# A gated linear recurrence: diagonal and five lower levels of the intra-chunk scores as four blocks of 32 keys by 32 queries

## The chip, the cores and the metric

The kernel runs on one core of a Trainium2 chip. The metric is the device time of one execution in microseconds (us). TensorE is written PE here, its weight loads PEld, VectorE DVE, ScalarE ACT, GpSimd POOL and the DMA-issuing engine SP, as the profile writes them.

## What is computed

One decoder layer over 1024 tokens of width 1024: a projection, a gated linear recurrence (HGRN2, 4 heads of 128 by 128) beside sliding-window attention, a gated merge, a layer norm and a mixture of 32 experts. The change lies in the recurrence alone. Per chunk of tokens it needs the scores

```python
def step(state, xs):
    qb, kb, vb, lb_c = xs
    b = jnp.cumsum(lb_c, axis=2)
    o_inter = jnp.einsum('bhtk,bhkv->bhtv', qb * jnp.exp(b), state)
    diff = b[:, :, :, None, :] - b[:, :, None, :, :]
    decay = jnp.exp(jnp.where(tri[:, :, None], diff, -jnp.inf))
    scores = jnp.einsum('bhtk,bhtsk,bhsk->bhts', qb, decay, kb)
    o_intra = jnp.einsum('bhts,bhsv->bhtv', scores, vb)
...
```

Scores exist only for keys that are not later than their query, so the matrix of a chunk (keys by queries) is upper triangular.

## The kernel before

The program has four stages: the attention with its projections (to about 300 us), the recurrence (about 305 to 550 us), the merge with norm and router (to about 800 us), and the experts. Through the attention and the recurrence a second piece of work is woven into PE's order: the stream, which multiplies the remaining columns of the projection as three matmuls of 512 columns each per step (lines 102 to 104). PE's order is written by the program (`pe_order`); the function `weave` puts a piece of the stream ahead of each group of the recurrence, by a fixed share of the stream and not by any clock. DVE, ACT, POOL and SP are ordered by a scheduler in these two stages.

The recurrence (`hgrn`) works on chunks of 128 tokens, eight of them. The triangle of a chunk is built by levels h = 64, 32, ..., 1 and a diagonal. At level h the chunk is cut into pairs of h tokens; the scores of the later half's queries against the earlier half's keys are one product of two decayed operands, which stand side by side in one tile e of 128 (channels) by 4 heads by 128 (tokens). `prep_level` makes e: on ACT two exponentials (lines 562 and 565), on DVE a subtraction, two multiplications and an addition (lines 564, 566, 569, 570); the addition turns the tile of sums `hl` into that of the next level, so that the levels of a chunk are made one after the other, h = 1 first. `level` multiplies: for each head e by itself on PE into a PSUM tile `pb` (keys on partitions, 4 heads by 128 queries), and then copies what belongs to the level into the scores `st` (tile `hst`, set to zero by POOL). Level 64 multiplies one block of 64 by 64 per head, level 32 two blocks of 32 by 32 per head (lines 580, 581), whose results lie in partitions 0 to 31 and 64 to 95, and ACT copies them. The levels 16, 8, 4, 2, 1 multiply 128 by 128 per head (line 583), and one DVE copy under a mask takes what counts (line 590). The diagonal does the same with keys and queries as they are (lines 549, 550).

Operands are in full 32-bit floating point, for which one matmul of the program stands as two MATMUL rows in the trace.

A group is prepared two groups before it is multiplied (`ahead = 2`). There are five `pb` buffers in PSUM, so a copy that is late holds one of five. After the levels come the decayed keys, the output and the state of the chunk (`decay`, `output`, `state`), which read the finished scores.

Of the kernel before, what the change touches and what calls it, by code (L numbers as in the profile page):

```python
# [7 lines left out]
I32 = mybir.dt.int32  # L8
# [14 lines left out]

LAST = (15, 23, 31)
ORDER = tuple(e for e in range(NE) if e not in LAST) + LAST
LEVELS = (64, 32, 16, 8, 4, 2, 1)


def constants():
# [12 lines left out]
    parts["tok"] = np.arange(8)[None, :] * 128 + r - FAR  # L42
    for h in LEVELS[2:]:
        parts[f"lev{h}"] = (r // (2 * h) == c // (2 * h)) & (r % (2 * h) < h) & (c % (2 * h) >= h)
# [16 lines left out]
class Builder:  # L61
# [457 lines left out]
    def hgrn(self):  # L519
# [3 lines left out]
        nc = self.nc  # L523
        mm = nc.tensor.matmul
        V = {}
        lo, hi = WHERE[f"lev{LEVELS[2]}"][0], WHERE["lev1"][1]
        lev = self.tile([128, hi - lo], F32, "lev", 1)
        nc.sync.dma_start(lev, self.a["const"][:, lo:hi])

        def mask(name):  # L530
            m = self.c("ident") if name == 0 else lev[:, WHERE[f"lev{name}"][0] - lo:WHERE[f"lev{name}"][1] - lo]
            return m.bitcast(I32)[:, None, :].to_broadcast([128, 4, 128])

        def load(n):
            t0 = slice(n * 128, n * 128 + 128)
            for nm, src in (("hl", self.hl[:, :, t0]), ("hk", self.hk[:, :, t0]), ("hq", self.hq[:, :, t0]),
# [2 lines left out]
                V[nm, n] = self.tile([128, 4, 128], F32, nm, 2)  # L539
                nc.sync.dma_start(V[nm, n], src)  # L540

        def prep_diag(n):
            V["st", n] = self.tile([128, 4, 128], F32, "hst", 1)
            nc.gpsimd.memset(V["st", n], 0.0)

        def diag(n):
            pp = self.bank("pb", (128, 4, 128))
            for hd in range(4):
                mm(pp[:, hd], V["hk", n][:, hd], V["hq", n][:, hd], start=True, stop=True)
            nc.vector.copy_predicated(V["st", n], mask(0), pp)  # L550

        def prep_level(n, h):
            q, kT, b = V["hq", n], V["hk", n], V["hl", n]
            ns = 4 * (64 // h)

            def view(t):
                return t.rearrange("p h (s two x) -> p (h s) two x", two=2, x=h)

            e = self.tile([128, 4, 128], F32, "hE", 2)
            ev, bv, qv, kv = view(e), view(b), view(q), view(kT)  # L560
            ref = bv[:, :, 0, h - 1:h].to_broadcast([128, ns, h])
            nc.scalar.activation(ev[:, :, 1], bv[:, :, 1], AF.Exp)
            if h > 1:
                nc.vector.tensor_sub(ev[:, :, 0], ref, bv[:, :, 0])
                nc.scalar.activation(ev[:, :, 0], ev[:, :, 0], AF.Exp)
                nc.vector.tensor_mul(ev[:, :, 0], ev[:, :, 0], kv[:, :, 0])
            else:
                nc.gpsimd.tensor_copy(ev[:, :, 0], kv[:, :, 0])
            nc.vector.tensor_mul(ev[:, :, 1], ev[:, :, 1], qv[:, :, 1])
            nc.vector.tensor_add(bv[:, :, 1], bv[:, :, 1], ref)  # L570
            V["e", n, h] = e

        def level(n, h):
            e, st = V.pop(("e", n, h)), V["st", n]
            pp = self.bank("pb", (128, 4, 128))
            for hd in range(4):
                if h == 64:
                    mm(pp[0:64, hd, 64:128], e[:, hd, 0:64], e[:, hd, 64:128], start=True, stop=True)
                elif h == 32:
                    mm(pp[0:32, hd, 32:64], e[:, hd, 0:32], e[:, hd, 32:64], start=True, stop=True)  # L580
                    mm(pp[64:96, hd, 96:128], e[:, hd, 64:96], e[:, hd, 96:128], start=True, stop=True)
                else:
                    mm(pp[:, hd], e[:, hd], e[:, hd], start=True, stop=True)
            if h == 64:
                nc.scalar.copy(st[0:64, :, 64:128], pp[0:64, :, 64:128])
            elif h == 32:
                nc.scalar.copy(st[0:32, :, 32:64], pp[0:32, :, 32:64])
                nc.scalar.copy(st[64:96, :, 96:128], pp[64:96, :, 96:128])
            else:
                nc.vector.copy_predicated(st, mask(h), pp)  # L590

        def prep_decay(n):
            b = V["hl", n]
# [56 lines left out]
        for n in range(8):  # L650
            at = 11 * n
            groups.append((at, lambda n=n: prep_diag(n), lambda n=n: diag(n)))
            for i, h in enumerate(reversed(LEVELS)):
                pre = lambda n=n, h=h: prep_level(n, h)
                if i == 3 and n < 7:
                    pre = lambda n=n, h=h: (load(n + 1), prep_level(n, h))
                groups.append((at + 1 + i, pre, lambda n=n, h=h: level(n, h)))
            groups.append((at + 8, lambda n=n: prep_decay(n), lambda n=n: decay(n)))
            groups.append((at + 10.5, none, lambda n=n: state(n)))
            groups.append((at + 9.6, none, lambda n=n: output(n)))  # L660
            groups.append((at + 13.5, none, lambda n=n: out(n)))
# [392 lines left out]
    def column(self, t, e):  # L1054

        x = ORDER[e]
        return t[:, x:x + 1]
# [35 lines left out]
    def fetch(self, first=False):  # L1093
# [4 lines left out]
        e, m, k = self.pieces[n]  # L1098
        x = ORDER[e]
        if m == "w_d":  # L1100
# [397 lines left out]
```

## Time and profile before

| | us |
|---|---|
| median of 3 runs | 1424.0 (1423.0 to 1429.07) |
| the profiled execution's own time | 1423.78 |
| its span, first to last instruction | 1421.9 |
| PE busy | 1359.1 (96%) |
| DVE busy | 1058.2 (74%) |
| ACT busy | 792.3 (56%) |

The span is 1.9 us shorter than the time of the same execution. Busy time counts an instruction from start to end; on PE and DVE the next one starts before the last has ended, so two starts stand closer than one duration, and what an instruction costs its engine is read from starts.

### The profile page before, as it was taken

What the parts mean: (1) busy time and instruction counts of PE and PEld (TensorE: products, weight loads), DVE (VectorE), ACT (ScalarE), POOL (GpSimd) and SP (SyncE); (2) the same over time, 40 slices, a digit from 0 to 9 for tenths busy, and PEclk for the clock granted to TensorE, in tenths of its full rate; (3) what the DMA queues carried; (4) which work ended last, traced back from release to release, by engine and by line L of the source; (5) the groups of instructions that cost most, each with busy time, mean ns of one, the idle gap of its engine ahead of it and who ended that gap; (6) DMA issues with size and microseconds to landing.
All of it is one profiled execution on the core that took longest, in us unless ns stands there. A gap on an engine that the chain in (4) does not pass through costs nothing. (4 is left out here: it accounts for less than half of the span.)

```text
span 1421.9 us, 20450 instructions
## 1 busy us (share of the span) xinstructions
PE 1359.1 (96%) x7162; PEld 1128.3 (79%) x7162; DVE 1058.2 (74%) x1654; ACT 792.3 (56%) x1282; POOL 239.6 (17%) x160
## 2 busy tenths in 40 slices
PE   7999999999999999999998999999999999999844
PEld 5888899988888888788787888888888888888721
DVE  4268977876666764857747889999999999999635
ACT  4367555434444442412201778888888888888533
POOL 0001221210010000410001112222222222222123
PEclk9999999999999999999999999999999999999967
DMA  6124223253334323774557899999999999999972
GB/s 254 56 89 156 88 92 105 67 173 116 126 108 136 111 88 103 240 252 137 174 195 277 314 361 369 370 359 349 360 349 359 357 359 360 360 359 361 370 264 95
DMA packets 142554, 327.68 MB, mean 230 GB/s; under 512 B 18614, under 2 KB 59702, under 8 KB 142448
## 3 DMA queue, kind: packets, MB, share of 16 engines
q1 hardware_dynamic: 132800, 308.78, 60.4%
q0 software_dynamic: 9648, 17.57, 4.8%
q8 instruction: 57, 0.93, 0.3%
q14 instruction: 49, 0.40, 0.1%
HBM read 291.43 MB, written 52.43 MB: 242 GB/s over the span
## 5 line engine op out<-in xcount | busy, mean ns | idle before, releaser
L98 DVE TENSOR_TENSOR el<-er,eh 128x1024 fp32r<-128x1024 f32 x368 | 436.5, 1221 | 53.7 <-ACT eh L97 38.1
L97 ACT CAST eh<-er 128x1024 fp32r<-128x1024 f32 x368 | 368.9, 1053 | 100.6 <-PE mm L103 83.5
L102 PE MATMUL mm<-xh,wh 128*128 128x512 f32 x480 | 198.3, 413 | 8.3 <-ACT wh L97 7.3
L102 PE MATMUL mm<-eh,xh 128*128 128x512 f32 x496 | 196.4, 396 | 0.0
L103 PE MATMUL mm<-el,xh 128*128 128x512 f32 x496 | 196.2, 395 | 0.0
L104 PE MATMUL mm<-eh,xl 128*128 128x512 f32 x496 | 196.1, 395 | 0.0
L103 PE MATMUL mm<-xl,wh 128*128 128x512 f32 x480 | 188.4, 393 | 0.8 <-DVE xl L98 0.8
L104 PE MATMUL mm<-xh,wl 128*128 128x512 f32 x480 | 189.0, 394 | 0.0
L104 PEld LDWEIGHTS mm<-eh,xl 128*128 128x128 f32 x496 | 93.2, 188 | 22.6
L103 PEld LDWEIGHTS mm<-el,xh 128*128 128x128 f32 x496 | 93.2, 188 | 22.3
L102 PEld LDWEIGHTS mm<-eh,xh 128*128 128x128 f32 x496 | 93.2, 188 | 22.3
L102 PEld LDWEIGHTS mm<-xh,wh 128*128 128x128 f32 x480 | 91.1, 190 | 24.2 <-ACT wh L97 7.3
L104 PEld LDWEIGHTS mm<-xh,wl 128*128 128x128 f32 x480 | 90.6, 189 | 20.6 <-DVE wl L98 0.8
L1064 POOL DMA_INDIRECT xg<-x1d,gi x32 | 58.1, 1814 | 279.3 <-PE pb L1127 236.3
L103 PEld LDWEIGHTS mm<-xl,wh 128*128 128x128 f32 x480 | 91.1, 190 | 16.0 <-DVE xl L98 1.4
L102 PE MATMUL mm<-eh,hth 128*128 128x512 f32 x240 | 100.2, 418 | 0.0
L1068 POOL DMA_INDIRECT zd<-y,gi x29 | 69.9, 2411 | 156.5 <-ACT y L1218 156.5
L104 PE MATMUL mm<-eh,htl 128*128 128x512 f32 x240 | 94.8, 395 | 0.0
L103 PE MATMUL mm<-el,hth 128*128 128x512 f32 x240 | 94.8, 395 | 0.0
L102 PE MATMUL mm<-wh,xh 128*128 128x256 f32 x256 | 73.1, 285 | 0.0
L104 PE MATMUL mm<-wh,xl 128*128 128x256 f32 x256 | 72.4, 283 | 0.0
L103 PE MATMUL mm<-wl,xh 128*128 128x256 f32 x256 | 72.4, 283 | 0.0
(257 smaller groups left out, 2566.6 us busy)
## 6 DMA issues: line engine op xcount, KB each, us to landing
er<-w_g SPq DMA_DIRECT2D x128, 512.0 KB, 12.5
er<-w_u SPq DMA_DIRECT2D x128, 512.0 KB, 12.5
er<-w_d SPq DMA_DIRECT2D x128, 512.0 KB, 12.0
wr<-w_in SPq DMA_DIRECT2D x38, 512.0 KB, 4.4
gated<-st SPq DMA_DIRECT2D x32, 256.0 KB, 2.1
st<-gated SPq DMA_DIRECT2D x32, 256.0 KB, 2.7
xr<-xt SPq DMA_DIRECT2D x8, 512.0 KB, 7.6
wab<-w_a SPq DMA_DIRECT2D x16, 256.0 KB, 3.7
```

Of the source, the lines that this page charges most:

```text
L97: self.nc.scalar.copy(hi, src)
L98: (eng or self.nc.vector).tensor_sub(lo, src, hi.bitcast(F32))
L102: mm(out, lh, rh, start=start, stop=False)
L103: mm(out, lh, rl, start=False, stop=False)
L104: mm(out, ll, rh, start=False, stop=stop)
L1064: self.nc.gpsimd.indirect_dma_start(to, None, rows, bass.IndirectOffsetOnAxis(ap=self.column(self.gi, e), axis=0), bounds_check=T - 1, oob ...
L1068: self.nc.gpsimd.indirect_dma_start(self.zd, bass.IndirectOffsetOnAxis(ap=idx, axis=0), y, None, bounds_check=T - 1, oob_is_err=False, com ...
```

## The change

The diagonal and the levels 16 to 1 no longer multiply 128 by 128 per head, but four blocks of 32 keys by 32 queries on the matrix's diagonal; no score of these levels lies outside those blocks. Each block writes its own 32 partitions of `pb`. The copy under the mask is cut the same way: four copies of 32 partitions by 4 heads by 32 queries.

```diff
+RUNS = [slice(b, b + 32) for b in range(0, 128, 32)]
...
-            return m.bitcast(I32)[:, None, :].to_broadcast([128, 4, 128])
+            return m.bitcast(I32)
+
+        def keep(st, name, pp):
+            for b in RUNS:
+                m = mask(name)[b, b][:, None, :].to_broadcast([32, 4, 32])
+                nc.vector.copy_predicated(st[b, :, b], m, pp[b, :, b])
...
+        def blocks(out, l, r):
+
+            for b in RUNS:
+                mm(out[b, b], l[:, b], r[:, b], start=True, stop=True)
...
-                mm(pp[:, hd], V["hk", n][:, hd], V["hq", n][:, hd], start=True, stop=True)
-            nc.vector.copy_predicated(V["st", n], mask(0), pp)
+                blocks(pp[:, hd], V["hk", n][:, hd], V["hq", n][:, hd])
+            keep(V["st", n], 0, pp)
...
-                    mm(pp[:, hd], e[:, hd], e[:, hd], start=True, stop=True)
+                    blocks(pp[:, hd], e[:, hd], e[:, hd])
...
-                nc.vector.copy_predicated(st, mask(h), pp)
+                keep(st, h, pp)
```

On PE the order of the groups is the same; a group of four matmuls has become one of sixteen. The first rows are PE's before, around a level of the first chunk, the second those of the change (line numbers have moved).

```order
L102 MATMUL mm<-xh,wh 128x512
L103 MATMUL mm<-xl,wh 128x512
L104 MATMUL mm<-xh,wl 128x512
L583 MATMUL pb<-hE 128x128 x4
L102 MATMUL mm<-xh,wh 128x512
```

```order
L103 MATMUL mm<-xh,wh 128x512
L104 MATMUL mm<-xl,wh 128x512
L105 MATMUL mm<-xh,wl 128x512
L551 MATMUL pb<-hE 32x32 x16
L103 MATMUL mm<-xh,wh 128x512
```

This is so at all 48 places; nothing of the stream has moved past a group.

On DVE the scheduler also shifts copies against the work for later levels. These are DVE's rows in the third chunk before, from the end of the preparation of level 2 on, and then those of the change at the same place (`hst` is written by the copies, `hE` is e, `st` is the stream's).

```order
L566 TENSOR_TENSOR hE<-hE,hk 128x128x2
L550 COPY_PREDICATED hst<-const,pb 128x512
L564 TENSOR_TENSOR hE<-hl 128x64x4
L590 COPY_PREDICATED hst<-lev,pb 128x512
L508 TENSOR_SCALAR st<-st 128x512
L566 TENSOR_TENSOR hE<-hE,hk 128x64x4
L569 TENSOR_TENSOR hE<-hE,hq 128x64x4
L570 TENSOR_TENSOR hl<-hl 128x64x4
L564 TENSOR_TENSOR hE<-hl 128x32x8
L590 COPY_PREDICATED hst<-lev,pb 128x512
```

```order
L577 TENSOR_TENSOR hE<-hE,hk 128x128x2
L538 COPY_PREDICATED hst<-const,pb 32x4x32 x4
L538 COPY_PREDICATED hst<-lev,pb 32x4x32 x4
L509 TENSOR_SCALAR st<-st 128x512
L575 TENSOR_TENSOR hE<-hl 128x64x4
L580 TENSOR_TENSOR hE<-hE,hq 128x64x4
L581 TENSOR_TENSOR hl<-hl 128x64x4
L577 TENSOR_TENSOR hE<-hE,hk 128x64x4
L538 COPY_PREDICATED hst<-lev,pb 32x4x32 x4
L575 TENSOR_TENSOR hE<-hl 128x32x8
```

The copies of level 1 now stand ahead of the first DVE step for level 4 (the tile of 64 pieces of 4), where one copy stood behind it.

## Rows read from the trace of the kernel before

**Rows 1.** The page: span, busy time by engine, granted clock in 40 slices.

```profile
span 1421.9 us, 20450 instructions
...
PE 1359.1 (96%) x7162; PEld 1128.3 (79%) x7162; DVE 1058.2 (74%) x1654; ACT 792.3 (56%) x1282; POOL 239.6 (17%) x160
...
PEclk9999999999999999999999999999999999999967
```

**Rows 2.** Stretches: length, busy PE, PEld, DVE, ACT, POOL (counts), clock, DMA share, GB/s.

```profile
350.00:380.00 30.00, 30.00 (x192) 25.67 (x191) 19.75 (x49) 13.47 (x30) 1.38 (x2) 1.00 0.40 124
...
550.00:600.00 50.00, 47.06 (x205) 36.71 (x205) 35.49 (x44) 16.70 (x20) 15.21 (x7) 1.00 0.66 208
800.00:1300.00 500.00, 500.00 (x2319) 407.35 (x2318) 452.55 (x442) 409.53 (x499) 116.06 (x54) 1.00 0.99 360
```

**Rows 3.** PE's waits from 290 to 560 us: in total, times, longest.

```profile
PE mm L102 <- ACT st L507: 0.7, 1, 0.7
```

**Rows 4.** Groups by line: count, then busy us, mean ns, and idle before.

```profile
L583 PE MATMUL pb<-hE 128*128 128x128 f32 x320 | 42.3, 275 | 0.0
...
L590 DVE COPY_PREDICATED hst<-lev,pb 128x512 f32<-128x512 int32 x40 | 29.6, 741 | 1.0 <-PE pb L583 0.8
...
L344 DVE COPY_PREDICATED as<-const,sc 128x256 f32<-128x256 int32 x28 | 10.9, 442 | 3.2 <-ACT as L340 3.1
```

**Rows 5.** Timeline of PE around a level of 128 by 128: start, length, instruction.

```profile
307.74 0.40 PE L104 MATMUL mm<-xh,wl 128*128 128x512 f32 x1
307.98 1.06 PE L583 MATMUL pb<-hE 128*128 128x128 f32 x8
...
309.11 0.39 PE L103 MATMUL mm<-xl,wh 128*128 128x512 f32 x1
309.34 0.39 PE L104 MATMUL mm<-xh,wl 128*128 128x512 f32 x1
```

**Rows 6.** Timeline of PE around a level 32.

```profile
321.15 0.39 PE L104 MATMUL mm<-xh,wl 128*128 128x512 f32 x1
...
321.52 0.20 PE L580 MATMUL pb<-hE 128*32 128x32 f32 x1
...
321.71 0.20 PE L580 MATMUL pb<-hE 128*32 128x32 f32 x1
321.72 0.20 PE L581 MATMUL pb<-hE 128*32 128x32 f32 x1
321.84 0.50 PE L102 MATMUL mm<-xh,wh 128*128 128x512 f32 x1
322.18 0.39 PE L103 MATMUL mm<-xl,wh 128*128 128x512 f32 x1
```

**Rows 7.** Timeline of DVE: copies under a mask, and 128-element operations on PSUM.

```profile
191.98 0.77 DVE L344 COPY_PREDICATED as<-const,sc 128x256 f32<-128x256 int32 x2
...
308.83 0.73 DVE L550 COPY_PREDICATED hst<-const,pb 128x512 f32<-128x512 int32 x1
309.45 0.41 DVE L564 TENSOR_TENSOR hE<-hl 128x256 f32<-128x256 f32 x1
...
364.04 1.13 DVE L642 SCALAR_TENSOR_TENSOR ho<-pb,hss,hg 128x128 f32<-128x128 f32 x4 [1.13 <-POOL hss L679]
```

**Rows 8.** Timeline of DVE and PE where the third chunk's levels begin.

```profile
365.08 0.41 DVE L569 TENSOR_TENSOR hE<-hE,hq 128x256 f32<-128x256 f32 x1
...
367.45 0.42 DVE L570 TENSOR_TENSOR hl<-hl 128x256 f32<-128x256 f32 x1
367.79 0.42 DVE L566 TENSOR_TENSOR hE<-hE,hk 128x256 f32<-128x256 f32 x1
...
366.52 1.06 PE L583 MATMUL pb<-hE 128*128 128x128 f32 x8
...
369.48 0.72 PE L583 MATMUL pb<-hE 128*128 128x128 f32 x5
```

**Rows 9.** PE's waits from 550 to 610 us, where the merge begins.

```profile
PE mm L104 <- DVE l L98: 2.2, 5, 0.5
```

## The prediction, made before the changed kernel ran

> **What bounds the kernel now.** I read the page first: PE is busy for 96% of a span of 1421.9 us, at a granted clock of nine tenths or more in all but the last two slices [rows 1]. An average says nothing of the recurrence, so the stretches come next. In 30 us inside it PE is busy for all 30.00, DVE for 19.75, ACT for 13.47, and the DMA engines for 0.40 of the time [rows 2]. Of that 30 us a chunk takes nearly the whole (eight chunks in some 245 us). Then PE's waits: between 290 and 560 us it waits once for another engine, for 0.7 us [rows 3]. The stage is bound by PE alone, and what its blocks cost is what the stage is worth. The reader should look at starts, not at durations: a MATMUL row of the levels is 275 ns long on average [rows 4], but eight of them take 1.06 us together [rows 5].
>
> What comes behind the recurrence is read from two stretches. From 800 to 1300 us PE is busy without a gap and the DMA engines to 0.99 [rows 2]. The experts' weights are fetched by steps of the merge, not at a time of their own, so a recurrence that ends earlier moves all of this earlier by as much.
>
> **PE: what a block costs now.** The last plain matmul before a level starts at 307.74, the second one behind it at 309.11 [rows 5]: 1.37 us. Two plain matmuls of the stream start 0.23 us apart (309.11 and 309.34 [rows 5]); two such steps belong to the stream, so the block costs 1.37 - 0.46 = 0.91 us. Line 583 has 320 rows [rows 4], eight to a block: 40 blocks, and the eight diagonals have the same shape. 48 blocks x 0.91 = 43.7 us of the stage.
>
> **PE: what a block will cost.** The trace of before has a near relative: level 32, which already multiplies 32 by 32 with 128 channels. Its two blocks per head write different partitions, so they use different 32 columns of the array. Measured the same way, from 321.15 to 322.18 [rows 6], it is 1.03 - 0.46 = 0.57 us for sixteen rows. How these sixteen run decides the case. Rows of line 580 alone go from 321.52 (its second) to 321.71 (its eighth): 0.19 / 6 = 0.032 us from one to the next in the same columns. The last of line 581 starts 0.01 us behind that of line 580 [rows 6]. So two column groups run side by side, each at 0.032 us a row. The eight rows of one column group thus take 8 x 0.032 = 0.26 us, and the remaining 0.31 us of the 0.57 are paid once, for entering and leaving the narrow shape.
>
> The changed block has 32 rows in four column groups: again eight rows in each. If four run side by side as two do, the block takes the 0.57 us of level 32 and two more offsets of 0.01: 0.59 us. It saves 0.91 - 0.59 = 0.32 us, and 48 x 0.32 = **15.4 us** on PE.
>
> What no row of before shows is three or four column groups at once. The bounds: if the offsets between groups cost nothing, 0.57, a saving of 16.3 us; if only two run at a time, eight more steps of 0.032, 0.83 us, a saving of 0.08 x 48 = 3.8 us. I take the first end, since the offset of 0.01 us leaves room for four within 0.032.
>
> The Trainium skill speaks against the change at this place: TensorEngine Tiling, Instruction Overhead, says that each matmul carries about 60 cycles, so that a free dimension of 1 costs as much as one of 60, and warns against taking a tiling factor from a dimension that is already small. As an estimate from that page, 60 cycles at 2.4 GHz are 25 ns, and 32 rows at 25 ns with the 0.31 us would be 1.11 us, 0.20 more than now. The rows of level 32 disagree in part: sixteen starts in 0.25 us are 16 ns each, less than the page's floor, though 32 ns within one column group.
>
> **DVE: what is added.** One copy of 512 elements a partition keeps DVE for 309.45 - 308.83 = 0.62 us [rows 7]; it becomes four of 128. Two copies of 256 take 0.77 us together [rows 7], one of them 0.44 by itself [rows 4], so the second starts 0.33 behind the first. From 256 to 512 it is 0.29 us, 1.13 ns an element; 128 elements would then take 0.33 - 0.145 = 0.19. From above, four operations of 128 elements from PSUM take 1.13 us at line 642 [rows 7], 0.26 from start to start. So four copies take 0.76 to 1.04 us, 0.14 to 0.42 more than now, or 48 times that, 7 to 20 us of DVE work. I take 0.8. The cover is DVE's idle third: about 10 us of each 30 [rows 2]; per chunk 6 x 0.14 to 0.42 = 0.8 to 2.5 us are added, and the chunk becomes 1.9 us shorter.
>
> An average cover can still fail where the levels follow each other closely. There DVE has per level four steps of 0.34 us (367.45 to 367.79 [rows 8]) and the copy: 1.36 + 0.8 = 2.16 us, 2.4 at the upper bound. Between two levels PE has six or nine plain matmuls: 6 x 0.23 + 0.59 = 1.97 or 9 x 0.23 + 0.59 = 2.66, on average 2.3. The two keep step; what guards PE is the lead with which e is ready. It is shortest in the third chunk: level 1 is ready at 365.49 and used at 366.52, level 2 at 368.21 and 369.48 [rows 8], leads of 1.0 and 1.3 us. Level 1 has one block and one copy between it and the output of the chunk before, which DVE waits for: its lead shrinks by 0.32 + 0.18 = 0.5 us; that of level 2 by twice as much, to 0.3. At the later levels of that chunk and in the other chunks the leads are longer. So DVE should not stop PE, or by a few tenths here and there; I charge **0.5 us** in all. A stall would first show at level 2 of a chunk.
>
> The scheduler's shifts on DVE cost nothing of their own: where copies now stand ahead of work for level 4, PE still has a whole level before it needs that. ACT, POOL and the bytes moved are unchanged; SP issues the same DMAs. The five PSUM buffers are held 0.2 us longer in turns of over 2 us. The semaphore at a block's end is still one.
>
> **The sum.** -15.4 + 0.5 = -14.9 us. The profiled execution took 1423.78 us (its span is 1421.9), 0.2 less than the median of 1424.0; 1424.0 - 14.9 = 1409.1, and I say **1409.0**. With the bounds of the block and of the small stalls (0 to 3) this case spans 1406 to 1413.
>
> **The rivals.** *Two column groups at a time.* The pattern of level 32 would be all the array does: 0.83 us a block, 1424.0 - 3.8 = 1420, within what can be measured. For it: no row shows more than two. Against it: nothing in the offset of 0.01 us says that two is an end.
>
> *One after another.* If the rows overlap in level 32 only because its two blocks lie 64 partitions apart, and neighbours do not, the 32 rows take 32 x 0.032 = 1.02 us and the block 1.33, 0.42 more than now: 48 x 0.42 = 20 us, **1444**. It decides from the point where a block costs more than 0.91, that is, above 19 ns a row. The rule of TensorEngine Tiling in the Trainium skill would end on this side too, by its estimate at 0.20 x 48 = 9.6 us slower. Against both: 16 ns a row in level 32 [rows 6].
>
> *DVE becomes the bound.* If copies of 32 partitions do not follow each other closely but each runs its full length of 0.44 us (the length of a 256-element copy [rows 4]), four take 1.77, a level 3.1 us against PE's 2.3. Over six such groups that is 4.8 us a chunk less a lead of about 2: some 2.8 x 8 = 22 us against 15.4 won, 1431. From about 1.3 us for four copies on the gain begins to shrink. Against it: two copies of 256 overlap [rows 7].
>
> *The gain stops at the merge.* From 550 to 600 us DMA is at 0.66 and PE waits 2.2 us for halves of weights [rows 2, 9]. Should those loads not start earlier with the recurrence's end, some of the 15 us turns into waits there; all of it would give 1424, a third 1414. Against it: the waits are at most 0.5 us each, and the loads are issued by groups of the recurrence.
>
> That the change does not do what it says can be left out: the order shows sixteen 32 by 32 matmuls at all 48 places.
>
> **The chances.** About 0.5%, 7 us, can be told from no change. Forecast 0.68; part of it lost to DVE or at the merge (1413 to 1418) 0.09; two at a time 0.11; all lost at the merge 0.04; one after another 0.05; DVE as the bound 0.03. Faster by over 0.5% (below 1417) is the forecast and most of the second: 0.76. Slower is the last two: 0.08. The rest, 0.16, is no change. For 8 in 10 the range must take in the forecast, the partial losses and half of the two-at-a-time case: 1405 to 1420; the forecast's own is 1406 to 1413.
>
> **What would show it.** In the changed profile the 128x32 rows of a block should start in four staggered lines, 8 ns or so apart, with 0.03 us within one line; the plain matmuls before and behind a block should stand 1.05 us apart by the measure above (0.59 + 0.46). The recurrence's PE should still be full, its waits under 1.5 us. DVE copies should start about 0.2 us apart. Matmul rows 16 ns or more apart mean two at a time, 32 ns one after another; PE waiting for `hE` from DVE in most chunks means the copies are dearer than thought; an unmoved first expert with a shorter recurrence means the merge took it.

## The result and the profile after

The changed kernel takes 1412.2 us, median of 4 runs (1410.6 to 1413.68), against 1424.3 before: a ratio of 0.9912, 95% interval 0.9891 to 0.9933, faster by 12.1 us where 14.9 were forecast. Its profiled execution took 1413.68 us with a span of 1411.5.

Three views of the changed kernel answer to those of before: from the page the span and the busy times [rows 1], two of the stretches [rows 2], and the waits of PE, here from 303 to 545 us [rows 3].

```profile
span 1411.5 us, 22907 instructions
...
PE 1347.8 (95%) x8314; PEld 1099.6 (78%) x8314; DVE 1083.8 (77%) x1798; ACT 790.0 (56%) x1282; POOL 243.3 (17%) x160
```

```profile
350.00:380.00 30.00, 29.50 (x349) 22.83 (x341) 23.55 (x67) 13.31 (x30) 2.23 (x4) 1.00 0.39 123
...
800.00:1300.00 500.00, 500.00 (x2324) 407.42 (x2323) 452.00 (x443) 407.95 (x497) 117.91 (x55) 1.00 0.99 359
```

```profile
PE pb L589 <- DVE hE L577: 1.1, 2, 0.7
PE pb L620 <- DVE hkT L608: 1.0, 2, 0.8
PE pb L551 <- DVE hE L577: 0.4, 1, 0.4
PE pb L551 <- issue: 0.2, 1, 0.2
```

PE is no longer full in the recurrence: it waits for DVE, for e (`hE`) and for the decayed keys (`hkT`), 2.5 us in the rows above. DVE's busy time in that 30 us went from 19.75 to 23.55.

**The block came out as worked out.** PE's timeline around the first level 1 after, to be laid beside [rows 5]:

```profile
308.59 0.40 PE L105 MATMUL mm<-xh,wl 128*128 128x512 f32 x1
308.92 0.46 PE L551 MATMUL pb<-hE 128*32 128x32 f32 x32
309.31 0.50 PE L103 MATMUL mm<-xh,wh 128*128 128x512 f32 x1
309.65 0.39 PE L104 MATMUL mm<-xl,wh 128*128 128x512 f32 x1
```

From 308.59 to 309.65 it is 1.06 us; less two steps of 0.23 that is 0.60, against 0.91 before and 0.59 forecast. All 32 rows lie within 0.46 us, and they start within 0.26 us, in this block as in each of the 48: four column groups do run side by side.

**The copies did not.** DVE's timeline near the end of the first chunk's levels:

```profile
317.59 1.28 DVE L538 COPY_PREDICATED hst<-lev,pb 32x128 f32<-32x128 int32 x4
318.91 0.43 DVE L575 TENSOR_TENSOR hE<-hl 128x256 f32<-128x256 f32 x1
...
320.37 1.28 DVE L538 COPY_PREDICATED hst<-lev,pb 32x128 f32<-32x128 int32 x4
321.68 0.43 DVE L509 TENSOR_SCALAR st<-st 128x512 f32<-128x512 f32 x1
322.03 0.42 DVE L575 TENSOR_TENSOR hE<-hl 128x256 f32<-128x256 f32 x1
...
323.03 0.42 DVE L577 TENSOR_TENSOR hE<-hE,hk 128x256 f32<-128x256 f32 x1
```

Four copies hold DVE from 317.59 to 318.91, 1.32 us, not 0.8. From one level's subtraction (318.91) to the next one's (322.03) DVE needs 3.1 us, where PE needs 2.0 or 2.7. So e for level 64, ready at 323.03 + 0.42 = 323.45, is late, and the same moment on PE reads:

```profile
322.51 0.40 PE L105 MATMUL mm<-xh,wl 128*128 128x512 f32 x1
323.60 0.65 PE L589 MATMUL pb<-hE 128*64 128x64 f32 x8 [0.69 <-DVE hE L577]
```

**Where the time went.** The recurrence is taken from the start of its first diagonal block to the start of its last transposition. It took 247.5 us before and 236.8 after, 10.7 less. In the profiled execution it also began 1.3 us later (306.9 against 305.6 us), before anything that the change touches; so the span fell by 10.4 us and not by more. Of the 15.4 us that 48 blocks should save, the recurrence shows 10.7. What became of the other 4.7 us is the subject of the experiments.

### The profile page after: what moved, and what is told of

Its sections match the earlier page's. It is cut to its first block, busy times and chain, and to the rows that moved or that the text cites. A ratio compares the mean times of both kernels' runs of the same rounds, so it can differ in the third digit from the quotient of the medians.

```text
span 1411.5 us, 22907 instructions
## 1 busy us (share of the span) xinstructions
PE 1347.8 (95%) x8314; PEld 1099.6 (78%) x8314; DVE 1083.8 (77%) x1798; ACT 790.0 (56%) x1282; POOL 243.3 (17%) x160
## 6 DMA issues: line engine op xcount, KB each, us to landing
er<-w_g SPq DMA_DIRECT2D x128, 512.0 KB, 12.1
```

## The experiments

The theory, H: a copy whose first partition differs from that of the instruction ahead of it waits until that one has ended. The copies then cost 1.3 us a group, DVE falls behind along a chunk, and PE waits. Its rivals: the scheduler's new order and not the length makes copies late (S); short copies never overlap, whatever their partitions (L); PE's waits are not what holds the gain back (D); chance (R). Ratios are to the kernel before in the same session, whose medians lay between 1423.4 and 1424.6 us.

| run | PE's blocks | DVE's copies of a group | recurrence, us | ratio (95% interval) |
|---|---|---|---|---|
| before | 128x128 | one, 128 partitions | 247.5 | 1 |
| the change | 32x32 | four of 32 partitions | 236.8 | 0.9912 (0.9891 to 0.9933) |
| again | same | same | 237.1 | 0.9950 (0.9936 to 0.9963) |
| again2 | same | same | 237.3 | 0.9920 (0.9905 to 0.9935) |
| compact_one | 32x32 | one of 128 | 233.4 | 0.9887 (0.9872 to 0.9902) |
| compact_four | 32x32 | the same one, four times | 233.4 | 0.9897 (0.9882 to 0.9912) |
| compact_quads | 32x32 | four of 32 | 239.2 | 0.9941 (0.9927 to 0.9955) |
| wide_quads | 128x128 | four of 32 | 248.5 | 1.0014 (1.0005 to 1.0023) |
| wide_full4 | 128x128 | four of 128 | 247.5 | 1.0002 (0.9992 to 1.0012) |
| pairs | 32x32, two levels together | one of 128 | 225.7 | 0.9840 (0.9827 to 0.9854) |
| pairs_quads | 32x32, two levels together | four of 32 | 236.3 | 0.9914 (0.9900 to 0.9928) |

### The changed kernel again: again, again2

No edit. What was expected of the first:

> The changed kernel once more, for a second trace of it. Theory H (a copy whose first partition differs from the one before it waits until that one has ended): copies 0.32 to 0.33 us apart again, PE waits of about 3 us in the recurrence again, and a ratio to before of 0.991 to 0.993. What varies between executions is the first 30 us (in the first trace PE lost 1.35 us there against before), not the recurrence: 236 to 237.5 us from its first block to its last transposition, against 247.4 before. If the stalls were chance (rival R), the recurrence would move by more than 1 us.

And of the second:

> The changed kernel a third time, since its two ratios to before (0.991 and 0.995) lie outside each other's intervals while the recurrences of the two traces agree to 0.3 us. If the difference belongs to the session (what lies outside the recurrence varied by 3 us between traces), the ratio falls between 0.990 and 0.996 and the recurrence again takes 236.5 to 237.5 us. If the stalls themselves vary, the recurrence of this trace differs by more than 1 us from those two.

Measured: medians 1416.5 and 1413.5 us. The recurrence agrees within 0.5 us over three traces, and in each level 64 waits 1.1 to 1.2 us for DVE and the transposition of `hkT` 1.0; the waits of the shorter levels vary. The waits are no chance: R falls. The ratio of the first repetition missed its expectation, and its interval does not meet that of the first result. In its trace what lies behind the recurrence took 870.6 us against 867.8 and 868.2 in the other two; among the eleven traces that part varies from 867.6 to 871.2 with no pattern by kernel. The granted clock goes with a part of the difference. In the trace of again it was at 0.5, the lower of its two levels (1.2 GHz), from 769.5 to 776.3 us, in the merge; in the other two it was at 1.0 there. Of all fifteen runs of this kernel, the six with a mean granted clock of at most 0.984, four of them from again, have a median of 1416.8 us, and the nine with 0.985 or 0.986 one of 1413.5. Whether that makes the whole difference stays open, since only one run of each has a trace. The recurrence is the steadier measure of the two.

### One copy by another layout: compact_one

All four blocks write the same 32 columns of the PSUM tile, in their own partitions; the scores of the short levels gather in a tile of 32 columns under masks of 32 columns, and ACT spreads it once per chunk.

```diff
-                mm(out[b, b], l[:, b], r[:, b], start=True, stop=True)
+                mm(out[b, 0:32], l[:, b], r[:, b], start=True, stop=True)
...
-            for b in RUNS:
-                m = mask(name)[b, b][:, None, :].to_broadcast([32, 4, 32])
-                nc.vector.copy_predicated(st[b, :, b], m, pp[b, :, b])
+            m = mask(name)[:, None, :].to_broadcast([128, 4, 32])
+            nc.vector.copy_predicated(st, m, pp[:, :, 0:32])
...
-                keep(st, h, pp)
+                keep(V["c", n], h, pp)
+                if h == 16:
+                    for b in RUNS:
+                        nc.scalar.copy(st[b, :, b], V["c", n][b])
```

> PE's blocks as in the change, but all four write the same 32 columns of the PSUM tile, so that one copy of 128 partitions by 4 heads by 32 queries takes a level into a compact tile; ACT spreads that into the scores once per chunk (four copies of 32 partitions). Theory H: one copy takes about 0.2 us from start to start, DVE has about 6.6 us less to do per chunk than in the change, PE does not wait for hE or hkT, the recurrence takes 233 to 234 us, and the ratio to the changed kernel is about 0.997 (3 to 4 us), to before about 0.989. Rival S (the stalls come from the order in which the scheduler put DVE's copies, not from their length): PE still waits 2 us or more. Rival D (PE's waits are not what holds the gain back): ratio to before 0.991 as the changed kernel's.

The recurrence takes 233.4 us as expected. The kernel takes 1408.4 us, 8.2 less than again in the same session, where 3 to 4 were expected; the recurrence accounts for 3.7 of them, the rest lies outside it. Its waits of PE from 303 to 545 us, and the stretch that stands above for the change:

```profile
PE mm L105 <- ACT st L510: 0.7, 1, 0.7
```

```profile
350.00:380.00 30.00, 30.00 (x348) 23.13 (x347) 18.64 (x50) 14.52 (x35) 2.24 (x5) 1.00 0.37 117
```

PE waits for nothing of DVE's and is full. Without the waits the recurrence is shorter by 236.8 - 233.4 = 3.4 us, more than the 2.5 us of named waits. Part of the rest is that a wait is counted from the end of the matmul ahead, 0.40 us behind its start, where a block that does not wait starts 0.33 us behind that (308.59 and 308.92 above). D falls. S is not decided by this, since DVE's order differs here as well.

### As many copies in the same layout: compact_quads, compact_four

```diff
-            m = mask(name)[:, None, :].to_broadcast([128, 4, 32])
-            nc.vector.copy_predicated(st, m, pp[:, :, 0:32])
+            for b in RUNS:
+                m = mask(name)[b, None, :].to_broadcast([32, 4, 32])
+                nc.vector.copy_predicated(st[b], m, pp[b, :, 0:32])
```

> As compact_one, but the copy of each level is cut into four of 32 partitions, each of 128 elements a partition. Theory H: copies start 0.32 to 0.33 us apart, PE waits as in the change or a little more, recurrence 236 to 237.5 us, ratio to before 0.991 to 0.993. Rival L (short copies under a mask do not overlap whatever their partitions): the same as H here, but then compact_four must look the same as this one.

The other one repeats the whole copy four times:

```diff
-            m = mask(name)[:, None, :].to_broadcast([128, 4, 32])
-            nc.vector.copy_predicated(st, m, pp[:, :, 0:32])
+            for _ in RUNS:
+                m = mask(name)[:, None, :].to_broadcast([128, 4, 32])
+                nc.vector.copy_predicated(st, m, pp[:, :, 0:32])
```

> As compact_one, but the one copy of a level is done four times over, each of all 128 partitions by 128 elements (three of them repeat what is there). As many instructions and as many elements a partition as compact_quads; only the first partition stays the same. Theory H: starts 0.20 to 0.21 us apart, 0.8 us a level, PE waits under 1 us, recurrence 233 to 235 us, ratio to before 0.989 to 0.990. Rival L: starts 0.32 us apart, and times as compact_quads.

Cut into quadrants the recurrence goes from 233.4 to 239.2 us, worse than the change itself and 1.7 us above what was expected, and the ratio of 0.9941 lies above the expected 0.993; done four times over it stays at 233.4. The groups of copies of compact_quads and of compact_four:

```profile
L540 DVE COPY_PREDICATED hc<-lev,pb 32x128 f32<-32x128 int32 x192 | 57.2, 298 | 5.7
```

```profile
L540 DVE COPY_PREDICATED hc<-lev,pb 128x128 f32<-128x128 int32 x192 | 57.8, 301 | 2.9 <-PE pb L553 2.0
```

192 copies of the same length, 0.30 us, and only the cut differs. These lines cannot show it: durations are equal, starts are not. The pair does not settle L cleanly either. The scheduler put the repeated copies singly between other work (each of those held DVE for 0.20 us), and where four did stand together, all onto the same elements, they were 0.34 us apart. The next pair has no such repeats.

### The copies alone: wide_quads, wide_full4

PE multiplies 128 by 128 again. wide_quads keeps the change's copies:

```diff
-            for b in RUNS:
-                mm(out[b, b], l[:, b], r[:, b], start=True, stop=True)
+            mm(out, l, r, start=True, stop=True)
```

> The other half of the change alone: PE multiplies 128 by 128 per head as before, DVE copies in four pieces of 32 partitions as in the change. Theory H: the copies again start 0.32 to 0.33 us apart, a level costs DVE 1.36 + 1.3 = 2.7 us against PE's 2.27 or 2.95, so PE waits somewhat, 1 to 4 us in all in the recurrence; the plain matmuls stay at 227 to 229 ns. Ratio to before 1.001 to 1.003. Rival D (PE's waits come only from PE being faster, the copies cost nothing): no waits, ratio 1.000.

wide_full4 also cuts by queries only, so that every copy begins at the first partition:

```diff
-                m = mask(name)[b, b][:, None, :].to_broadcast([32, 4, 32])
-                nc.vector.copy_predicated(st[b, :, b], m, pp[b, :, b])
+                m = mask(name)[:, None, b].to_broadcast([128, 4, 32])
+                nc.vector.copy_predicated(st[:, :, b], m, pp[:, :, b])
```

> PE as before; DVE copies in four pieces, each of all 128 partitions by 4 heads by 32 queries, so that the first partition never changes. Theory H: starts 0.20 us apart, 0.8 us a group, no waits of PE, recurrence 247.4 to 247.6 us, ratio to before 1.000. Rival L (short copies do not overlap): 0.32 us apart and as wide_quads.

DVE's timeline at the fourth chunk, of wide_quads and then of wide_full4:

```profile
397.98 1.29 DVE L538 COPY_PREDICATED hst<-const,pb 32x128 f32<-32x128 int32 x4
399.29 0.42 DVE L574 TENSOR_TENSOR hE<-hl 128x256 f32<-128x256 f32 x1
```

```profile
397.75 0.89 DVE L538 COPY_PREDICATED hst<-const,pb 128x128 f32<-128x128 int32 x4
398.54 0.42 DVE L574 TENSOR_TENSOR hE<-hl 128x256 f32<-128x256 f32 x1
```

The same elements per partition, the same count, four times as many partitions: 1.31 us against 0.79 from the first copy to the instruction behind. L falls. The single copy takes 0.30 us either way; what differs is that the next one starts 0.1 us before its end, or 0.03 us behind it. This holds for all 145 copies that stand behind another copy, in either kernel. A semaphore does not make the difference: 93 of the 145 in wide_quads and 92 in wide_full4 carry a wait on DVE's own semaphore, and those without one behave as those with it.

Beside PE's old pace the 0.5 to 0.7 us more per group are nearly hidden: wide_quads loses 1.0 us in the recurrence and has a ratio as expected. PE's named waits for DVE, 0.2 us for `hkT`, are below the expected 1 to 4, and the rest is spread over starts.

In these two kernels DVE's order in the recurrence is the same, instruction by instruction (535 of them), so the 1.0 us comes from the length of the copies and not from the order. For the 3.4 us at PE's new pace no two runs have one order and two lengths; there S is argued against and not tested. The argument is from the change's trace: from 306.9 us until e for level 64 is ready at 323.45 DVE has no gap above 0.05 us, and five groups of copies fall into that time. As an estimate, at 0.79 us a group instead of 1.31 the same order would be done 2.6 us earlier, and the wait was 0.69 us.

The Trainium skill has a rule for this: VectorE: DVE Perf Modes, Two Vector instructions with no wait between them, says that an instruction starts only when every earlier Vector instruction has finished, if it reads or writes a memory (SBUF or PSUM) from another quadrant (32 partitions) than the last one that read or wrote that memory. The pair above agrees, and so do the copies of the change: 0.326 us from start to start in the median.

By that rule it is not the instruction ahead that counts, as in H, but the last one that touched the same memory. The first copies of the groups tell the two apart. Taken in the program's order, such a copy starts at the first partition, as does the instruction ahead of it, which has all 128. In the change's trace the eight of the diagonals, before which an operation on 128 partitions had last read PSUM, start 0.08 us before the end of the instruction ahead. Those of the levels, before which a copy from partition 96 had last read PSUM, start 0.03 us behind that end, all 35 of them. H as it was put does not give this, and the rule of the Trainium skill does. The eight also show that 32 partitions as such do not prevent the overlap.

### Two levels together: pairs, pairs_quads

The levels 1 and 2, 4 and 8, 16 and 32 stand together in PE's order, in compact_one's layout. Since there are fewer groups, the merge's first steps are inserted at other counts from the end (12, 8 and 5 instead of 16, 11 and 7); the lines below do not show that.

```diff
-            for i, h in enumerate(reversed(LEVELS)):
+            for i, hs in enumerate(((1, 2), (4, 8), (16, 32), (64,))):
...
+                def mains(n=n, hs=hs):
+                    for h in hs:
+                        level(n, h)
+                groups.append((at + 1.5 + 2 * i - (i == 3) * 0.5, pre, mains))
```

> compact_one with the levels 1 and 2, 4 and 8, 16 and 32 multiplied right behind each other, without matmuls of the stream between them. If 0.31 us of a narrow block are paid once for entering and leaving the narrow shape, three of seven such payments per chunk go: 8 x 3 x 0.31 = 7.4 us, recurrence about 226 to 228 us, ratio to before 0.983 to 0.985, provided that DVE, which must now deliver two levels at a time, keeps PE fed; up to 4 us may come back as waits for hE. If the 0.31 us belong to every block whatever stands beside it, the time is that of compact_one, 0.989.

1401.5 us, below both kernels by 22 and 11 us. PE's timeline around the levels 4 and 8 of the first chunk:

```profile
309.13 0.40 PE L107 MATMUL mm<-xh,wl 128*128 128x512 f32 x1
309.46 0.76 PE L552 MATMUL pb<-hE 128*32 128x32 f32 x64
310.15 0.50 PE L105 MATMUL mm<-xh,wh 128*128 128x512 f32 x1
310.49 0.40 PE L106 MATMUL mm<-xl,wh 128*128 128x512 f32 x1
```

1.36 - 0.46 = 0.90 us for two levels, 0.60 for one: the second costs 0.30, and the other 0.30 are paid once for the change of shape. The recurrence fell by 7.7 us against the 7.4 of 24 such payments.

Then with the copies cut into quadrants again, by the same edit as compact_quads:

> The pairs kernel with the copies cut into four quadrants again. PE then needs about 7 us less for the recurrence than in compact_one, DVE as much as in the change. Theory H: DVE is now what the levels wait for; PE waits 5 to 12 us for hE and hkT, and the recurrence stays at 232 to 238 us instead of 225.7: the gain of pairing is mostly lost, ratio to before 0.988 to 0.992. If the copies were hidden behind PE, the recurrence would take 226 us and the ratio 0.984.

The recurrence is 236.3 us, 10.6 more than with one copy, and about what the change has without pairing. PE's waits from 303 to 545 us:

```profile
PE pb L553 <- DVE hE L581: 3.5, 3, 1.7
PE pb L595 <- DVE hE L581: 2.1, 3, 1.0
PE mm L105 <- ACT st L510: 0.7, 1, 0.7
PE pb L627 <- DVE hkT L615: 0.5, 1, 0.5
PE pb L593 <- DVE hE L581: 0.4, 1, 0.4
```

The named waits for DVE, 6.5 us, do not cover the 10.6. The mean step between plain matmuls is 233.5 ns here and 229.1 in pairs, which over 581 steps is 2.6 us more. That is the granted clock, the third number from the end of each of these stretches:

```profile
395.00:399.00 4.00, 2.44 (x41) 1.69 (x39) 3.95 (x13) 1.96 (x5) 0.00 (x0) 1.00 0.00 0
399.34:402.75 3.41, 3.41 (x23) 2.76 (x19) 2.80 (x10) 2.72 (x9) 0.19 (x2) 0.50 0.48 147
```

PE was busy for 2.44 of 4 us while it waited for DVE; then for 3.4 us the clock was at 0.50, the lower of its two levels (1.2 GHz), and plain matmuls started 427 ns apart instead of 227. The same stands at 488.1 to 491.5 us, behind 4 us with PE busy for 2.08. No other kernel here has the lower level within its recurrence. If the long waits made it fall, which this trace suggests and no run was made to show, they cost PE more than their own length; about 1.5 us of the 10.6 stay without a name. With PE this fast the copies by quadrants are the stage's bound: what PE saves is given back to DVE.

## Why the prediction was right, and where it was off

**The block: right.** 0.59 us forecast, 0.60 measured. Reading level 32 as eight rows per column group, and not as sixteen rows, gave it. The rivals "two column groups at a time" and "one after another" fall with it, and so does the 1.11 us estimated from the Trainium skill (TensorEngine Tiling (Array Packing), Instruction Overhead): the trace shows 32 ns a row in one column group, but 8 ns over four.

**DVE's added work: the term that was mis-sized.** The step "four copies take 0.76 to 1.04 us" holds for copies of 128 partitions: wide_full4 has 0.79. For 32 partitions each it was 1.31, outside the bounds. I took the spacing from instructions that all start at the first partition [rows 7], and the copies of the change do not. A row of before showed it, on DVE's timeline in the attention, where line 327 reads and writes now the lower and now the upper half of the partitions:

```profile
192.78 0.91 DVE L327 TENSOR_TENSOR ksl<-ak,ksh 64x128 fp32r<-64x128 f32 x3
```

Three of 0.29 us in 0.91 us: not one overlaps. That row and not line 642 was the nearest relative. My own text gave 1.3 us as the point from which the gain begins to shrink, and it was at 1.3. It is the mechanism of the rival "DVE becomes the bound", which I gave 0.03, at a lower price: each copy does run its full length, but that is 0.30 us and not the 0.44 of a copy of 256 elements. Of the signs named beforehand two failed for it: copies 0.2 us apart (0.326), and waits of PE under 1.5 us (2.5).

**The stalls: right kind, wrong size and place.** I charged 0.5 us, with 3 as the upper end; compact_one shows 3.4. They fell on level 64 and on `hkT`, late in a chunk, and on levels 4 and 8 of the third chunk; the first was level 64 of the first chunk, and in that trace level 2 never waited. With 3.1 us a level on DVE against 2.0 to 2.7 on PE, the lead does not grow along a chunk, it is used up. I compared an average PE step with a DVE step without the stream's work.

**Not in the sum.** Plain matmuls behind a narrow block start further apart: 228.3 ns in the mean before, 230.1 after, over 533 steps 1.0 us. Before, too, the four steps behind the first one after level 32 were 231, 236, 228 and 232 ns; I took the stream's step as constant. With the stalls (3.4) and some 0.3 us because the blocks of before cost 0.903 us on average and not 0.91, this makes up the 4.7 us that the recurrence fell short of 15.4.

**The merge: right.** PE's wait for halves of weights from 550 to 600 us fell to 1.2 us from 2.2 [rows 9]:

```profile
PE mm L105 <- DVE l L99: 1.2, 3, 0.5
```

The rest of the program moved along: the part behind the recurrence took 867.8 us after, 868.8 before.

**The number: in part luck.** The first result, 1412.2, lies in the forecast's own case, 1406 to 1413, by 0.8 us. The repetitions, 1416.5 and 1413.5, lie in the case beside it, in which a part of the gain is lost to DVE or at the merge (1413 to 1418), and to which I gave 0.09 against 0.68. By the mechanism that second case is what happened: 3.4 us went to DVE. All three lie within 1405 to 1420.

## What to carry to other kernels

When an operation is cut into pieces over partitions, price each engine by rows whose pieces also change their first partition: PE gained from it (four column groups side by side), DVE lost the overlap between instructions. Let the narrow products land in the same columns, so that one copy over all partitions serves them. And group narrow products together: the change of shape costs as much as one of them.

## What was not expected of the hardware

Four copies of 32 partitions held DVE longer (1.31 us) than four of 128 partitions with the same elements each (0.79 us), though each lasts 0.30 us. The first copy of a level was late too, though the instruction ahead began at the same partition. Entering and leaving the narrow shape on PE cost 0.30 us, once for one level and once for two together. In pairs_quads the granted clock fell to 0.50 for 3.4 us behind PE's waits, twice. Plain matmuls of 512 columns behind narrow blocks stood, after a first step of 0.34 us, mostly 231 to 236 ns apart instead of 227 for about five steps (236 in the mean at the third step behind the diagonal blocks); the mean step was 230.1 to 230.2 ns in all six traces with single narrow blocks, stalls or not, against 228.3 before. Its cause was not sought.
